# A hybrid decoder layer: TensorE's instructions in written order through the banded attention, with other banks for two of its tiles

## The chip, the core and the metric

The kernel runs on one core of one Trainium2 chip. The metric is the device time of one launch in microseconds. The core's engines work through queues of their own and wait for one another by semaphores: TensorE (PE in the profile) does matmuls and transposes into the accumulators (PSUM, eight banks of 128 x 512 float32), ScalarE (ACT) and VectorE (DVE) read these, GpSimd (POOL) does a little arithmetic and starts some DMAs, and SyncE (SP) starts the loads of the weights.

## What is computed

One layer of a decoder with 256 tokens of width 2048. The part that the change touches is the mixer:

```
c_q, c_kv, k_r, q_s, k_s, v_s, gates = split(h @ w_in)
q  = rms_norm(c_q) @ mla_w_q_up          # latent attention, dense and causal
kv = rms_norm(c_kv) @ mla_w_kv_up
o_a = mla_attention(q, kv, rope(k_r))
o_b = swa_attention(q_s, k_s, v_s, sinks, rel_table)
      # 32 query heads of 64 in 4 groups, one key and value head for each group,
      # window 128 in banded blocks, bias by distance, a learned sink in the softmax
y  = (sigmoid(gA) * (o_a @ w_o_mla) + sigmoid(gB) * (o_b @ w_o_swa)) @ w_out
```

Behind it come the residual sum, a norm and a feed-forward part with a short convolution; neither is touched. The results have to be those of float32, so each large product is made of three matmuls of operands that are split into a high and a low part (float32r): high x high, low x high, high x low.

## The kernel before

**Projections.** `gemm` computes 512 (or 320) columns of `h @ w_in` for both blocks of 128 tokens, over 16 slices of depth. Weights come in chunks of two slices (`wchunk`): a DMA into a tile raw, ScalarE's cast into whi (L129), VectorE's subtraction into wlo (L130), all from small rings of tiles; then 12 matmuls (`mm3`, L154 to L156) add into accg, two accumulator banks of the pool `pacc`, which has four. The other pools of banks are `pst` (tag "t", two) and `pss` (tag "s", two).

**Ticks.** After each chunk `gemm` calls `tick`, which runs the steps that `at(t, ...)` has put down for that tick. So the small work of the attention is written between the chunks of a projection that runs at the same time.

**The banded attention.** Sixteen units u of two heads each, four units to a group g. While the projection of the next group runs, the four units of a group come one by one, two ticks apart. Of a unit are written, in this order and at these ticks:

- `swa_qT` (L454 ff., tile xp): four transposes of the scaled queries, copied to x2 by ScalarE;
- `score` (tile s, L490 and L492): six matmuls; VectorE adds the bias and takes the maxima; then `stats`, `expo` (ScalarE's exponentials, L512) and `norm` (ScalarE L522, VectorE L524);
- `pt` (L471): twice three transposes of the probabilities, each group split by ScalarE (L233, tile pth) and VectorE (L234, tile ptl);
- `pv` (tile po, L538 to L541): four matmuls with the values, copied and added by ScalarE (L543) and VectorE (L546) to o.

**The latent part.** Behind the last group the same manner of work goes on beside the projections of c_q (cq), of c_kv with k_r (ck, kr), and of the gates B, columns 0 and 1 (`gate_b(0)`, `gate_b(1)`). `latent` copies the accumulator (L579), squares it in place for the norm (L580, with the accumulator as scratch), scales it (L587), and `tr` transposes it (L593): a tile cqT0, cqT1 or ckT in one bank takes two pairs of transposes, and behind each pair stands a split of what it wrote, ScalarE's high part (L236) and VectorE's low part (L237):

```
for j in range(2):
    for t in range(NT):
        pe.transpose(pt[:, j * 256 + t * P:j * 256 + (t + 1) * P], lat[t][...], ident)
    c = slice(j * 256, (j + 1) * 256)
    split_to(hi_t[p][:, c], lo_t[p][:, c], pt[:, c], gmat[...])
```

**What sets the order.** The program is written in the order of ticks, but a scheduler of the compiler places each engine's instructions; it lets work that it holds ready go ahead of work that waits. Only a `tc.manual_schedule(engines=...)` around a piece of the program makes it keep the written order for the engines named; before, that is used at the head alone, for VectorE, ScalarE and SyncE. An instruction that waits stops all that is behind it on its engine.

Of the kernel before, what the change touches and what calls it, by code (L numbers as in the profile page):

```python
# [11 lines left out]
F32 = mybir.dt.float32  # L12
F32R = mybir.dt.float32r
# [6 lines left out]
P = 128  # L20
# [21 lines left out]
def trunk_layer(ctx, tc, x, g_mix_post, g_ffn_post, w_in, w_q, w_kv, sinks, wo_a, wo_b, w_out, w_up, w_down,  # L42
# [9 lines left out]
    pacc = ctx.enter_context(tc.tile_pool(name="pacc", bufs=4, space=PS))  # L52
    pss = ctx.enter_context(tc.tile_pool(name="pss", bufs=2, space=PS))
    pst = ctx.enter_context(tc.tile_pool(name="pst", bufs=2, space=PS))
# [4 lines left out]
    def sb(pl, shape, name, dt=F32, tag=None, bufs=None):  # L59
        return pl.tile(shape, dt, name=name, tag=tag or name, **({"bufs": bufs} if bufs else {}))  # L60
# [73 lines left out]
    steps = defaultdict(list)  # L134
    now = [0]

    def at(t, *fs):
        steps[max(t, now[0])].extend(fs)

    def tick():  # L140
        for f in steps.pop(now[0], ()):
            f()
        now[0] += 1

    def drain():
        while steps:
            tick()
# [97 lines left out]
    def bias_load(u, q):  # L245
        b = bias_of[u] = sb(pb, [P, 2, 384], f"bias{u}", tag="bias", bufs=2)
        row = lambda n: bass.AP(strip.tensor, strip.offset + 2 * u * 384, [[1, P], [384, 2], [1, n]])
        q.dma_start(b[:, :, 0:256], row(256))
        q.dma_start(b[:, :, 256:384], row(128))
# [196 lines left out]
    def swa_q(g, acc):  # L446

        qx_of[g] = []
        for t in range(NT):
            q = sb(p1, [P, 8, 2, 64], f"qx{g}_{t}", F32R, tag="qx", bufs=2)  # L450
            a3 = acc[t].rearrange("p (a b) -> p a b", b=64)
            split_to(q[:, :, 0, :], q[:, :, 1, :], a3, r1s[:, t:t + 1])
            qx_of[g].append(q)

    def swa_qT(u):

        qx, i = qx_of[u // 4], u % 4
        pt = pst.tile([P, 512], F32R, name=f"xp{u}", tag="t")
        for j in range(2):
            for t in range(NT):  # L460
                pe.transpose(pt[:, (j * 2 + t) * P:(j * 2 + t + 1) * P],
                             qx[t][:, 2 * i + j, :, :].rearrange("p a b -> p (a b)"), ident_r)
        xt = sb(p1, [P, 512], f"x2{u}", F32R, tag="x2", bufs=3)
        act.copy(xt, pt.bitcast(F32))
        xs_of[u] = xt

    def p_transpose(p, dst, tag):

        pt = pst.tile([P, 512], F32, name=f"pt{tag}", tag="t")
        for j, c in enumerate((2, 0, 1)):  # L470
            pe.transpose(pt[:, j * P:(j + 1) * P], p[:, c * P:(c + 1) * P], ident)  # L471
        split_to(dst[0], dst[1], pt[:, 0:384])

    def swa_unit(u, t0):

        g = u // 4
        h0 = 2 * u
        st = {}

        def load():  # L480
            if u > 1:
                bias_load(u, pool)
            st["bias"] = bias_of[u]
            st["p"] = sb(p1, [P, 2, 384], f"p{u}", tag="p", bufs=3)
            st["mx"] = sb(p1, [P, 2, 2], f"mx{u}", tag="mx", bufs=3)

        def score(i):
            sp = pss.tile([P, 512], F32, name=f"s{u}_{i}", tag="s")
            q = xs_of[u][:, i * 256:(i + 1) * 256]
            pe.matmul(sp[:, 0:256].rearrange("p (a b) -> p a b", a=2), q[:, 0:P], kx[g][:, :, P:2 * P], start=True, stop=True)  # L490
            for w in (1, 0):
                pe.matmul(sp[:, 256:512], q[:, P:2 * P], kx[g][:, w, P:384], start=w == 1, stop=w == 0)  # L492
            p, bias, mx = st["p"][:, i, :], st["bias"][:, i, :], st["mx"]
            vec.tensor_tensor(p[:, 0:P], sp[:, P:256], bias[:, 0:P], op=ALU.add)
            vec.tensor_tensor_reduce(p[:, P:384], sp[:, 256:512], bias[:, P:384], op0=ALU.add, op1=ALU.min, scale=-1.0, scalar=-NEG, accum_out=mx[:, i, 1:2])
            vec.tensor_tensor_reduce(p[:, 0:P], p[:, 0:P], sp[:, 0:P], op0=ALU.add, op1=ALU.min, scale=-1.0, scalar=-NEG, accum_out=mx[:, i, 0:1])

        def stats():
            mx = st["mx"]
            sk = sink[:, h0:h0 + 2].unsqueeze(2).to_broadcast([P, 2, 2])  # L500
            vec.tensor_tensor(mx, mx, sk, op=ALU.min)
            if u == 0:
                sb(p1, [P, 24], "pad_d")
            st["e"] = sb(p1, [P, 2, 2], f"e{u}", tag="e", bufs=3)
            vec.tensor_tensor(st["e"], mx, sk, op=ALU.subtract)
            st["sm"] = sb(p1, [P, 2, 2], f"sm{u}", tag="sm", bufs=3)
            act.activation(st["e"], st["e"], AF.Exp)

        def expo(i):
            pb = st["p"]  # L510
            for t, (a, b) in enumerate(((0, 128), (128, 384))):
                act.activation(pb[:, i, a:b], pb[:, i, a:b], AF.Exp, bias=st["mx"][:, i, t:t + 1], scale=-1.0,  # L512
                               accum_out=st["sm"][:, i, t:t + 1])

        def norm():
            pb, sm = st["p"], st["sm"]
            vec.tensor_tensor(sm, sm, st["e"], op=ALU.add)
            vec.reciprocal(sm, sm)
            for i in range(2):
                for t, (a, b) in enumerate(((0, 128), (128, 384))):  # L520
                    if i:
                        act.activation(pb[:, i, a:b], pb[:, i, a:b], AF.Copy, scale=sm[:, i, t:t + 1])  # L522
                    else:
                        vec.tensor_scalar(pb[:, i, a:b], pb[:, i, a:b], sm[:, i, t:t + 1], None, op0=ALU.mult)  # L524

        def pt(i):
            if i == 0:
                st["pt"] = [sb(p1, [P, 2, 384], f"pt{part}{u}", F32R, tag="pt" + part, bufs=2) for part in "hl"]
            p_transpose(st["p"][:, i, :], [w_[:, i, :] for w_ in st["pt"]], f"{u}_{i}")

        def pv():

            st["po"] = pst.tile([P, 512], F32, name=f"po{u}", tag="t")
            st["o"] = sb(p1, [P, 256], f"o{u}", tag="o", bufs=2)
            v0, v1 = (vx[t][:, g, :, :].rearrange("p a b -> p (a b)") for t in range(NT))
            po = st["po"].rearrange("p (a b) -> p a b", a=2)
            ph, pl_ = st["pt"]
            pe.matmul(po, v0, ph[:, :, P:384], start=True, stop=False)  # L538
            pe.matmul(po[:, :, P:256], v1, ph[:, :, 0:P], start=False, stop=False)
            pe.matmul(po[:, :, P:256], v1, pl_[:, :, 0:P], start=False, stop=False)  # L540
            pe.matmul(po, v0, pl_[:, :, P:384], start=False, stop=True)  # L541
            cr = sb(p1, [64, 512], f"cr{u}", tag="cr", bufs=1)
            act.copy(cr, st["po"][64:128, :])  # L543
            for j in range(2):
                c = slice(j * 256, (j + 1) * 256)
                vec.tensor_tensor(st["o"][j * 64:(j + 1) * 64, :], st["po"][0:64, c], cr[:, c], op=ALU.add)  # L546
            act.copy(OH(u), st["o"])
            pool.tensor_tensor(OL(u), st["o"], OH(u).bitcast(F32), op=ALU.subtract)

        at(t0 - (3 if u > 1 else 1), load)  # L550
        at(t0, lambda: score(0), lambda: score(1))
        at(t0 + 1, stats, lambda: expo(0), lambda: expo(1), norm)
        at(t0 + 3, lambda: pt(0), lambda: pt(1))
        at(t0 + 4, pv)

    for g in range(4):
        if g:
            more_raw[:] = late
            accq, _ = gemm(XH, XL, w_in, 0, KT, C_QS + 512 * g, 512)
        else:  # L560
            kv_evac(acckv)
        swa_q(g, accq)
        b = now[0]
        for i in range(4):
            at(b + 1 + 2 * i, lambda u=4 * g + i: swa_qT(u))
            swa_unit(4 * g + i, b + 2 + 2 * i)


# [40 lines left out]
    acc, _ = gemm(XH, XL, w_in, 0, KT, 0, 512)  # L609
# [4 lines left out]
    acc, _ = gemm(XH, XL, w_in, 0, KT, C_KV, KVR + ROPE)  # L614
# [38 lines left out]

    tb = {0: gate_b(0), 1: gate_b(1)}
    drain()
    es1.close()
    esb.close()

# [143 lines left out]
    b = now[0] + 42  # L802
# [11 lines left out]
    for j in range(4):  # L814
        acc, _ = gemm(XH, XL, w_in, 0, KT, C_GA + 512 * j, 512)
        for t in range(NT):
            g = stg(f"ta{j}_{t}")
# [48 lines left out]
    for j in range(4):  # L866
        ld = merge_loads(j)
        acc, _ = gemm(AH, AL, wo_a, 0, KT, 512 * j, 512)
        for t in range(NT):
            a, b = ld[t]  # L870
# [63 lines left out]
    for b in range(4):  # L934
        c0, n = W_BLOCKS[b]
        last = b == 3
        acc, todo = gemm(MH_, ML_, w_out, 0, KT, c0, n, split=0 if last else None, extra={i: (px,) for i in range(EXTRA)} if last else None)
# [115 lines left out]
    for j in range(4):  # L1053
        acc, _ = down(0, 24, 512 * j, 512)
# [32 lines left out]
    for b in range(4):  # L1087
# [5 lines left out]
        acc, todo = down(24, 20, 512 * b, 512, split=5 if last else None)  # L1093
# [74 lines left out]
```

## Time and profile before

| | before |
|---|---|
| median of 3 runs | 1477.67 us (1477.65 to 1477.79) |
| the profiled execution's own time | 1478.18 us |
| its span, first to last instruction | 1476.4 us |
| TensorE busy | 1463.9 us, 99% of the span |
| VectorE, ScalarE, GpSimd busy | 66%, 54%, 4% |
| mean granted clock of TensorE | 0.998 |
| the banded attention, 50.89 to 195.56 us | 144.67 us, ScalarE busy 84% of it |

The profile is that of one execution. Busy time is the time in which an engine had an instruction in work; a matmul's record is longer than its share of the stream, since matmuls overlap, so a price per matmul is read from the distance of two starts. A wait has a length and a releaser, the instruction whose end let it go. Stretches are given in microseconds from the first instruction.

### The profile page before, as it was taken

What the parts mean: (1) busy time and instruction counts of PE and PEld (TensorE: products, weight loads), DVE (VectorE), ACT (ScalarE), POOL (GpSimd) and SP (SyncE); (2) the same over time, 40 slices, a digit from 0 to 9 for tenths busy, and PEclk for the clock granted to TensorE, in tenths of its full rate; (3) what the DMA queues carried; (4) which work ended last, traced back from release to release, by engine and by line L of the source; (5) the groups of instructions that cost most, each with busy time, mean ns of one, the idle gap of its engine ahead of it and who ended that gap; (6) DMA issues with size and microseconds to landing.
All of it is one profiled execution on the core that took longest, in us unless ns stands there. A gap on an engine that the chain in (4) does not pass through costs nothing.

```text
span 1476.4 us, 20927 instructions
## 1 busy us (share of the span) xinstructions
PE 1463.9 (99%) x7694; PEld 1255.4 (85%) x7694; DVE 973.5 (66%) x1730; ACT 804.1 (54%) x1328; POOL 54.3 (4%) x88
## 2 busy tenths in 40 slices
PE   9999999999999999999999999999999999999997
PEld 7888888888899988888888888888888888888886
DVE  7688784445667665655777687776444676688555
ACT  7588864434565554344665465554443555555443
POOL 0022200000000010000000000000000000000000
PEclk9999999999999999999999999999999999999999
DMA  9665566666655557776655655656555655655653
GB/s 350 191 174 137 134 196 197 203 211 200 186 160 155 176 168 244 260 238 225 200 172 171 210 181 186 191 181 207 197 189 190 191 178 182 214 186 184 201 195 119
DMA packets 160935, 285.41 MB, mean 193 GB/s; under 512 B 18560, under 2 KB 31488, under 8 KB 160704
## 3 DMA queue, kind: packets, MB, share of 16 engines
q1 hardware_dynamic: 155904, 268.45, 56.9%
q0 software_dynamic: 4496, 14.95, 4.1%
q8 instruction: 60, 0.98, 0.3%
q10 hardware_dynamic: 432, 0.68, 0.1%
q14 instruction: 43, 0.35, 0.1%
HBM read 277.74 MB, written 6.29 MB: 192 GB/s over the span
## 4 chain that ended last, share of the span: by engine, by line
PE 97%; ACT 1%; DMA 1%; DVE 1%; SPq 0%; issue 0%; DVEq 0%; ACTq 0%
PE accg L154 18%; PE accg L156 18%; PE accg L155 18%; PE accb L195 11%; PE acca L195 10%; PE accb L203 6%; PE acca L203 5%; PE acckv L339 1%; PE accq L339 1%; PE mpo L790 1%; PE ms L756 1%; PE pt L471 1%; PE qn L721 1%; PE qn L720 1%; PE qn L719 1%; PE s L492 0%
## 5 line engine op out<-in xcount | busy, mean ns | idle before, releaser
L130 DVE TENSOR_TENSOR wlo<-raw,whi 128x1024 fp32r<-128x1024 f32 (+1 forms) x484 | 587.4, 1217 | 426.6 <-ACT whi L129 400.1
L129 ACT CAST whi<-raw 128x1024 fp32r<-128x1024 f32 (+1 forms) x484 | 506.6, 1048 | 542.3 <-PE accg L156 318.7
L154 PE MATMUL accg<-whi,ah 128*128 128x512 f32 (+1 forms) x800 | 312.4, 391 | 0.0
L155 PE MATMUL accg<-wlo,ah 128*128 128x512 f32 (+1 forms) x800 | 310.4, 388 | 0.0
L156 PE MATMUL accg<-whi,al 128*128 128x512 f32 (+1 forms) x800 | 310.0, 387 | 0.0
L156 PEld LDWEIGHTS accg<-whi,al 128*128 128x128 f32 x800 | 150.2, 188 | 29.8
L155 PEld LDWEIGHTS accg<-wlo,ah 128*128 128x128 f32 x800 | 150.4, 188 | 27.7
L154 PEld LDWEIGHTS accg<-whi,ah 128*128 128x128 f32 x800 | 150.4, 188 | 27.4
L154 PE MATMUL accg<-whi,bh 128*128 128x512 f32 x272 | 106.6, 392 | 0.0
L156 PE MATMUL accg<-whi,bl 128*128 128x512 f32 x272 | 106.1, 390 | 0.0
L155 PE MATMUL accg<-wlo,bh 128*128 128x512 f32 x272 | 106.0, 390 | 0.0
L195 PE MATMUL accb<-bh,whi 128*128 128x512 f32 x352 | 84.2, 391 | 0.0
L195 PE MATMUL accb<-bl,whi 128*128 128x512 f32 x352 | 84.0, 390 | 0.0
L195 PEld LDWEIGHTS accb<-bh,whi 128*128 128x128 f32 x352 | 65.2, 188 | 13.3 <-ACT rfrow L931 0.3
L195 PEld LDWEIGHTS accb<-bl,whi 128*128 128x128 f32 x352 | 65.2, 188 | 13.0
L195 PE MATMUL acca<-bh,whi 128*128 128x512 f32 x320 | 76.2, 390 | 0.0
L195 PE MATMUL acca<-bl,whi 128*128 128x512 f32 x320 | 76.1, 390 | 0.0
L195 PEld LDWEIGHTS acca<-bh,whi 128*128 128x128 f32 x320 | 59.4, 188 | 12.2 <-DVE ds L1056 0.3
L195 PEld LDWEIGHTS acca<-bl,whi 128*128 128x128 f32 x320 | 59.4, 188 | 11.9
L156 PEld LDWEIGHTS accg<-whi,bl 128*128 128x128 f32 x272 | 51.1, 188 | 10.7
L154 PEld LDWEIGHTS accg<-whi,bh 128*128 128x128 f32 x272 | 51.1, 188 | 10.3
L155 PEld LDWEIGHTS accg<-wlo,bh 128*128 128x128 f32 x272 | 51.1, 188 | 10.2
(333 smaller groups left out, 1999.1 us busy)
## 6 DMA issues: line engine op xcount, KB each, us to landing
raw<-in_ffn_w_up_dram SPq DMA_DIRECT2D x176, 512.0 KB, 4.4
raw<-in_w_in_dram SPq DMA_DIRECT2D x96, 512.0 KB, 4.4
raw<-in_ffn_w_down_dram SPq DMA_DIRECT2D x88, 512.0 KB, 3.9
raw<-in_w_o_swa_dram SPq DMA_DIRECT2D x32, 512.0 KB, 4.3
raw<-in_w_o_mla_dram SPq DMA_DIRECT2D x32, 512.0 KB, 4.4
raw<-in_w_out_dram SPq DMA_DIRECT2D x32, 512.0 KB, 4.3
wxr<-in_w_in_dram SPq DMA_DIRECT2D x13, 512.0 KB, 7.8
raw<-in_mla_w_q_up_dram SPq DMA_DIRECT2D x48, 128.0 KB, 2.8
```

What stands on the lines that cost most here:

```text
L129: act.copy(hi[:, :n], raw[:, :n])
L130: vec.tensor_tensor(lo[:, :n], raw[:, :n], hi[:, :n].bitcast(F32), op=ALU.subtract)
L154: pe.matmul(o, ah, bh, start=start, stop=False)
L155: pe.matmul(o, ah, bl, start=False, stop=False)
L156: pe.matmul(o, al, bh, start=False, stop=stop)
L195: pe.matmul(acc[i], hi[:, c:c + P], xs(kt), start=kt == 0, stop=kt == nk - 1)
L203: pe.matmul(acc[i][:, 0:256], lo[:, c:c + P], xs(k + 2 * n + j)[:, 0:256], start=False, stop=False)
L339: pe.matmul(o(a)[t][:, c], xs[x_][t], w_[:, 512 * a + c.start:512 * a + c.stop], start=start, stop=stop)
L471: pe.transpose(pt[:, j * P:(j + 1) * P], p[:, c * P:(c + 1) * P], ident)
L719: pe.matmul(o, wh, ch(k), start=k == 0, stop=False)
L720: pe.matmul(o, wh, cl(k), start=False, stop=False)
L721: pe.matmul(o, wl, ch(k), start=False, stop=k == nk - 1)
```

## The change

`at` takes a turn, and a tick's steps run sorted by it. The query transposes of a unit (turn 1) move from one tick ahead of its scores to two ticks ahead (one for the first unit of a group), the value products get turn 2, and so an even tick writes the scores of one unit, the query transposes of the next and the value products of the unit two before, in this order. The tiles xp and po move from the pool `pst` to `pacc`, whose four banks also hold the running projection. And from the first group to behind `gate_b(1)` TensorE keeps the written order, in the latent part too; the other engines' order is still the scheduler's.

```diff
-    def at(t, *fs):
-        steps[max(t, now[0])].extend(fs)
+    def at(t, *fs, turn=0):
+        steps[max(t, now[0])].extend((turn, f) for f in fs)
...
-        for f in steps.pop(now[0], ()):
+        for _, f in sorted(steps.pop(now[0], ()), key=lambda e: e[0]):
             f()
...
-        pt = pst.tile([P, 512], F32R, name=f"xp{u}", tag="t")
+        pt = pacc.tile([P, 512], F32R, name=f"xp{u}", tag="acc")
...
-            st["po"] = pst.tile([P, 512], F32, name=f"po{u}", tag="t")
+            st["po"] = pacc.tile([P, 512], F32, name=f"po{u}", tag="acc")
...
-        at(t0 + 4, pv)
-
+        at(t0 + 4, pv, turn=2)
+
+    written = ExitStack()
+    written.enter_context(tc.manual_schedule(engines={mybir.EngineType.PE}))
     for g in range(4):
...
-            at(b + 1 + 2 * i, lambda u=4 * g + i: swa_qT(u))
+            at(b + (2 * i if i else 1), lambda u=4 * g + i: swa_qT(u), turn=1)
             swa_unit(4 * g + i, b + 2 + 2 * i)
...
     tb = {0: gate_b(0), 1: gate_b(1)}
     drain()
+    written.close()
```

First place, TensorE in a steady unit of the second group. Before, the two groups of probability transposes of unit 4 stand with a matmul of the projection between them, and behind ten more come the query transposes of unit 6, a matmul again and the value products (a name's number is its unit or chunk; the last number is the tile's own):

```order
L471 MATMUL pt4_0_1245<-ident_105,p4_1016 128x128 x3
L154 MATMUL accg_8_0_967<-whi14_1286,ah6_142 128x512
L471 MATMUL pt4_1_1251<-ident_105,p4_1016 128x128 x3
L155 MATMUL accg_8_0_967<-wlo14_1287,ah6_142 128x512
...
L461 MATMUL xp6_1272<-ident_r_110,qx1_0_961 128x128
L461 MATMUL xp6_1272<-ident_r_110,qx1_1_964 128x128
...
L156 MATMUL accg_8_1_968<-whi14_1286,al6_150 128x512
L538 MATMUL po4_1302<-pth4_1243,vx0_583 128x512
L539 MATMUL po4_1302<-pth4_1243,vx1_584 128x2x128
```

Now the even tick's bunch holds the scores of unit 6, the transposes of unit 7 (the two rows left out repeat the two shown) and the products of unit 4, and a whole chunk of 12 accg follows:

```order
L156 MATMUL accg_8_1_970<-whi14_1288,al6_150 128x512
L490 MATMUL s6_0_1304<-kx1_580,x26_1220 128x256
L492 MATMUL s6_0_1304<-kx1_580,x26_1220 128x256 x2
L490 MATMUL s6_1_1311<-kx1_580,x26_1220 128x256
L492 MATMUL s6_1_1311<-kx1_580,x26_1220 128x256 x2
L461 MATMUL xp7_1318<-ident_r_110,qx1_0_963 128x128
L461 MATMUL xp7_1318<-ident_r_110,qx1_1_966 128x128
...
L538 MATMUL po4_1325<-pth4_1252,vx0_583 128x512
L539 MATMUL po4_1325<-pth4_1252,vx1_584 128x2x128
L540 MATMUL po4_1325<-ptl4_1253,vx1_584 128x2x128
L541 MATMUL po4_1325<-ptl4_1253,vx0_583 128x512
```

The six pt of a unit stand together in the odd tick in the same way; small work that was spread over some five places of a unit is at two.

Second place, TensorE where the latent part's transposes stand. Before, the first pair of cqT0 and the second of cqT1 share a place, other matmuls stand between the pairs of one tile, and the second pair of cqT0 follows a chunk and a half later:

```order
L156 MATMUL accg_32_1_2250<-whi38_2472,al6_150 128x320
L540 MATMUL po15_2422<-ptl15_2391,vx1_584 128x2x128
L541 MATMUL po15_2422<-ptl15_2391,vx0_583 128x512
L593 MATMUL cqT0_2434<-ident_105,cq0_2227 128x128
L593 MATMUL cqT0_2434<-ident_105,cq1_2230 128x128
L593 MATMUL cqT1_2461<-ident_105,cq0_2227 128x128
L593 MATMUL cqT1_2461<-ident_105,cq1_2230 128x128
L154 MATMUL accg_32_0_2249<-whi38_2472,ah6_142 128x320
```

Now the four of cqT1 stand side by side behind the last matmul of chunk 37 (the two rows left out, the second pair, read as the first), with chunk 38 behind them:

```order
L156 MATMUL accg_32_1_2252<-whi37_2447,al5_149 128x320
L595 MATMUL cqT1_2463<-ident_105,cq0_2229 128x128
L595 MATMUL cqT1_2463<-ident_105,cq1_2232 128x128
...
L154 MATMUL accg_32_0_2251<-whi38_2474,ah6_142 128x320
L155 MATMUL accg_32_0_2251<-wlo38_2475,ah6_142 128x320
```

The same holds for cqT0, one chunk earlier, and for ckT, behind the last matmul of chunk 45.

Third place, ScalarE at the same transposes, whose high splits L236 are the first step to the second pair's release. Before, its queue there has the first split of cqT1 ahead of two casts, and the next two splits ahead of the cast of chunk 42:

```order
L236 ACTIVATE cqh_1808<-cqT1_2461,gx_123 128x256
L129 CAST whi40_2549<-raw40_2547 128x1024
L129 CAST whi41_2567<-raw41_2565 128x1024
L543 COPY cr15_2428<-po15_2422 64x512
L236 ACTIVATE cqh_1808<-cqT0_2434,gx_123 128x256
...
L129 CAST whi42_2585<-raw42_2583 128x1024
```

Now it reads:

```order
L236 ACTIVATE cqh_1810<-cqT0_2424,gx_123 128x256
L129 CAST whi40_2551<-raw40_2549 128x1024
...
L129 CAST whi41_2569<-raw41_2567 128x1024
L543 COPY cr15_2439<-po15_2433 64x512
L129 CAST whi42_2587<-raw42_2585 128x1024
L236 ACTIVATE cqh_1810<-cqT1_2463,gx_123 128x256
L547 CAST bh7_593<-o15_2434 128x256
```

The cast of chunk 42 has moved ahead of both splits of cqT1.

## Rows read from the trace of the kernel before

**Rows 1.** The page, engines: busy us, share of the span, instructions.

```profile
PE 1463.9 (99%) x7694; PEld 1255.4 (85%) x7694; DVE 973.5 (66%) x1730; ACT 804.1 (54%) x1328; POOL 54.3 (4%) x88
```

**Rows 2.** TensorE's waits: us in total, times, longest.

```profile
PE ckT L593 <- DVE ckx L237: 1.3, 1, 1.3
PE warm L69 <- DVE first L66: 1.1, 1, 1.1
```

**Rows 3.** Stretches: us, busy (x count) of five engines, clock, DMA share, GB/s.

```profile
50.89:195.56 144.67, 144.42 (x813) 122.84 (x812) 120.26 (x384) 121.92 (x316) 34.12 (x43) 1.00 0.59 158
215.00:222.00 7.00, 5.75 (x28) 4.42 (x27) 4.43 (x6) 3.89 (x5) 0.00 (x0) 1.00 0.76 232
222.00:361.00 139.00, 139.00 (x615) 115.09 (x614) 65.82 (x58) 58.80 (x59) 3.29 (x6) 1.00 0.65 204
...
1469.80:1476.40 6.60, 0.00 (x0) 0.00 (x0) 2.78 (x5) 0.00 (x0) 0.00 (x0) 0.50 0.43 160
```

**Rows 4.** TensorE's timeline of one unit: start, us, line, tiles, count.

```profile
100.35 0.46 PE L461 MATMUL xp<-ident_r,qx 128*128 128x128 f32 x4
100.65 0.47 PE L156 MATMUL accg<-whi,al 128*128 128x512 f32 x1
100.95 0.39 PE L538 MATMUL po<-pth,vx 128*128 128x512 f32 x1
...
101.64 0.40 PE L154 MATMUL accg<-whi,ah 128*128 128x512 f32 x1
...
103.26 0.28 PE L490 MATMUL s<-kx,x 128*128 128x256 f32 x1
...
103.98 0.40 PE L155 MATMUL accg<-wlo,ah 128*128 128x512 f32 x1
...
105.14 0.49 PE L471 MATMUL pt<-ident,p 128*128 128x128 f32 x3
105.39 0.48 PE L154 MATMUL accg<-whi,ah 128*128 128x512 f32 x1
105.71 0.49 PE L471 MATMUL pt<-ident,p 128*128 128x128 f32 x3
105.95 0.48 PE L155 MATMUL accg<-wlo,ah 128*128 128x512 f32 x1
106.27 0.39 PE L156 MATMUL accg<-whi,al 128*128 128x512 f32 x1
...
108.35 0.46 PE L461 MATMUL xp<-ident_r,qx 128*128 128x128 f32 x4
```

**Rows 5.** Timeline of all engines at ckT, accg left out; idle before, releaser.

```profile
215.55 0.38 PE L593 MATMUL ckT<-ident,ck 128*128 128x128 f32 x2
...
217.19 1.05 ACT L129 CAST whi<-raw 128x1024 fp32r<-128x1024 f32 x1 [0.84 <-DMA raw<-in_w_in_dram]
...
218.15 0.47 ACT L236 ACTIVATE ckx<-ckT,gx 128x256 fp32r<-128x256 f32 x1
218.27 1.23 DVE L130 TENSOR_TENSOR wlo<-raw,whi 128x1024 fp32r<-128x1024 f32 x1 [0.67 <-ACT whi L129]
219.42 0.48 DVE L237 SCALAR_TENSOR_TENSOR ckx<-ckT,gx,ckx 128x256 fp32r<-128x256 f32 x1
...
219.95 0.33 PE L593 MATMUL ckT<-ident,ck 128*128 128x128 f32 x1 [1.25 <-DVE ckx L237]
```

**Rows 6.** Timelines of ScalarE and VectorE in the latent part.

```profile
183.28 0.58 ACT L580 ACTIVATE accg<-cq 128x512 f32<-128x512 f32 x1
...
190.62 0.88 DVE L587 TENSOR_SCALAR cq<-cq,cq_y 128x512 f32<-128x512 f32 x2
```

**Rows 7.** The page, DMA issues: count, KB each, median us to landing.

```profile
raw<-in_w_in_dram SPq DMA_DIRECT2D x96, 512.0 KB, 4.4
```

**Rows 8.** TensorE's timeline at the head.

```profile
4.20 1.19 PE L339 MATMUL acckv<-whi,ah 128*128 128x256 f32 x4
...
5.81 0.63 PE L339 MATMUL acckv<-wlo,ah 128*128 128x512 f32 x2
6.28 0.64 PE L339 MATMUL accq<-whi,ah 128*128 128x256 f32 x4
```

## The prediction

> **What bounds the kernel now.** I read the page's busy list first: TensorE is busy in 99% of the span [rows 1]. The list of TensorE's waits says the same from the other side: over 1476 us its only wait of more than a microsecond, apart from that for the first operand at the start, is 1.3 us ahead of the second pair of ckT transposes, released by VectorE's low-part split [rows 2]. So time is added wherever TensorE is made to wait, and is won only where its own stream gets denser; there is no slack later that could swallow either. The table of stretches shows where the change acts: from 50.89 to 195.56 us, the banded attention beside the projections, TensorE is busy in 144.42 of 144.67 us, ScalarE in 121.92 (84%) and VectorE in 120.26; the plain gate projections behind it, 222 to 361 us, run 615 matmuls in 139.00 us, 0.226 us each, at granted clock 1.00 [rows 3].
>
> **What the bunches can win.** One steady unit of two heads is read from TensorE's timeline, from one query transpose xp to the next: 100.35 to 108.35, 8.00 us [rows 4]. In it stand 24 accg matmuls of 512 columns (24 x 0.226 = 5.42) and 20 small ones, which take the other 2.58. The group of four po goes by without loss (100.95 to 101.64, 0.69), and so do the six s (103.26 to 103.98, 0.72). A loss shows where accg follows transposes: the accg behind xp holds the engine for 0.30 us (100.65 to 100.95), and those behind pt for 0.32 (105.39 to 105.71, and 105.95 to 106.27), where 0.226 is usual [rows 4]. After the change a unit has two bunches, s-xp-po and pt-pt. The accg behind xp goes, but then po stands behind xp; one of two accg behind pt goes, but the first group of three pt takes only 0.25, so that some of the 0.09 is merely time of the transposes shown at the next instruction. I take 0.1 us a unit, 1.5 us for 16 units. The ends: nothing, and, if everything above the small groups' own pace went (xp 0.30, pt 2 x 0.25, s 0.72, po 0.69 and 5.42, together 7.63 of 8.00), 0.37 x 16 = 5.9. **Term: -1.5 (0 to -5.9).**
>
> **Does a fixed order make TensorE wait inside the units?** With the order written, everything queued behind a waiting instruction waits too, accg included. I followed each small group to what makes its operand. s needs ScalarE's copy of xp, which now has two chunks of accg instead of one (a chunk is 12 x 0.226 = 2.7 us). po stands one chunk and a bunch's start behind pt, about 3.9 us, and needs two splits on ScalarE and VectorE, some 1.4 us beyond pt. pt stands more than a chunk behind the normalisation. By the durations of one unit I get 2.5 us to spare ahead of po and 3.7 ahead of pt. The banks: xp and po now use the two accumulator banks that the running projection doesn't hold, and at each of three group ends the next projection takes both. It then waits for the xp copy and for po's two adds; there I count 0.3 to 0.9 us to spare. So zero for the units and group ends; if the cover is short, that is the third rival.
>
> **Where I expect waits: the latent part, with its pairs.** The four transposes of cqT0, cqT1 and ckT each stand in two pairs in one bank: the second pair is written only when ScalarE's high and VectorE's low split of the first have read it. Before, the scheduler put other matmuls between the pairs: in all three cases but ckT enough, at ckT one chunk, and 1.25 us were missing. There the whole chain can be read: pair one at 215.55; ScalarE's weight cast at 217.19, queued ahead, then the high split at 218.15; VectorE's weight split at 218.27, then the low split at 219.42; pair two at 219.95 [rows 5]. Now the four stand side by side, and TensorE pays the chain itself, three times.
>
> - **cqT0**: ScalarE's and VectorE's queues hold its splits right behind earlier work, with no weight chunk that waits for TensorE. The bare chain is 0.47 + 0.48 [rows 5] and about 0.25 of handing over and of the pair itself: **+1.2** (1.2 to 2.3, with another cast of 1.05 ahead).
> - **cqT1**: ahead of its high split ScalarE has the cast of chunk 42, which needs a ring slot that chunk 37 frees, and the last matmul of chunk 37 stands directly ahead of cqT1. So cast 1.05, weight split 1.23 and low split 0.48, about 2.7 [rows 5]. Chunk 42's data can be later still: a load takes 4.4 us to land [rows 7] and is issued when VectorE is done with chunk 39; by that I get 3.75. **+3.2** (1.2 to 4.5).
> - **ckT**: again the cast of a chunk (50) is queued ahead of the split, and needs the slot of chunk 45, whose last matmul is directly ahead of ckT. By the row above 2.7 if the data is there. In the trace the cast started only at 217.19, on data, and by the same chain the wait would be 4.2; but the two waits at cqT give the loads several us to catch up. 2.7 less the 1.25 of before: **+1.45** (-0.05 to +2.95).
>
> Two more that the fixed order uncovers. **po13** takes a bank that the projection cq held and that ScalarE still uses as scratch for the squares (0.58 us each, behind the two casts and in turn with exponentials [rows 6]); I get the first square 0.9 us after TensorE comes to po13: **+1.0** (0 to 1.5). **pt15** needs the normalisation of unit 15, which VectorE does behind the two scalings of cq (0.88) [rows 6]; before, the scheduler had let accg pass: **+0.3** (0 to 1.0).
>
> Outside this stretch TensorE's order is the same, and the moved steps (query transposes, value products) issue no DMA, so nothing is counted there or on SyncE's and GpSimd's queues. The bank moves alone cost nothing: the two banks that xp and po leave serve pt, kT and krT alone.
>
> **Sum**: -1.5 + 1.2 + 3.2 + 1.45 + 1.0 + 0.3 = +5.65 us on the profiled 1478.18 gives 1483.8; the median of the runs, 1477.67, stands 0.5 below the profiled one, so **1483.3 us**. The waits alone lie between +2.3 (three bare chains less 1.25) and +12.
>
> **Rivals.** (1) *The clock falls in the new waits.* It was 1.00 through ckT's 1.25 us, and 0.50 behind the last matmul, 1469.80 to 1476.40 [rows 3]. What a fall costs is bounded by the head: TensorE's first work follows a wait of 1.1 us [rows 2], four 256-column matmuls take 0.99 us from 4.20, and from 5.81 two of 512 take 0.47, the full rate [rows 8]. At most 4.7 us at half rate, 2.3 lost a fall; one or two make 1485.6 to 1487.9. A wait of 3 us is longer than any that I saw at full clock, but matmuls are dense on both sides of it. [...] Chance 0.10. (2) *The chains are short*: the other engines run ahead, po13 and pt15 are free, each pair waits the bare 1.2: 3 x 1.2 - 1.25 - 1.5 = +0.85, 1478.5, no change. For it speaks that ScalarE's queue order is the scheduler's, with idle time in the tail; against it, both casts named above need TensorE's last chunk. 0.17. (3) *ScalarE falls behind in the units*: it is used 84% on the mean, and if each unit is 0.3 us late for po or pt, 16 x 0.3 = 4.8 comes on top of the waits: 1488. It decides once the 2.5 us ahead of po is used up. 0.07. (4) *The dense stream wins*: 4.5 to 5.9 us from the bunches with bare chains gives 1477.67 + 2.35 - 5.2 = 1474.8, and lower only if a chain is hidden: the other side. It decides if a change between small and large matmuls costs 0.3 us a unit instead of 0.1. 0.06.
>
> **How the numbers follow.** Forecast 0.60, rivals 0.10, 0.17, 0.07, 0.06. What the measurement can tell from no change is about 0.2%, 3 us: faster means below 1474.7, slower above 1480.6. Rival 4 is half faster, half same; the forecast's lower tail (waits near 1.2 with po13 free) adds 0.03 to same. Faster 0.04, same 0.21, slower 0.75. The range leaves out rival 4, the lower half of rival 2, and the far ends of 3: 1478 to 1488.
>
> **What would show it.** In the profile after: TensorE's waits list cqT twice and ckT once, released by VectorE's low split, of 1 to 4 us each, and po13 released by ScalarE's square; a unit takes 7.9 instead of 8.00 us; no wait at s, xp, po, pt of units 1 to 12; PEclk 1.00 behind each wait. I am wrong if the waits sum to under 3 us, if the unit shrinks by over 0.25, or if waits show inside the units.

## The result and the profile after

The changed kernel takes **1488.95 us** (median of 6 runs, 1487.38 to 1490.29) where the kernel before takes 1477.73 (median of 6, beside them): ratio **1.0072**, 95% interval 1.0062 to 1.0082. It is slower, as forecast, but by 11.2 us where 5.65 was forecast, and 0.95 us beyond the upper end of the range.

The profiled execution took 1487.67 us. Its busy list, beside that of [rows 1], shows the same work and a longer span, 1485.9:

```profile
PE 1464.7 (99%) x7694; PEld 1259.1 (85%) x7694; DVE 979.3 (66%) x1730; ACT 803.4 (54%) x1328; POOL 56.9 (4%) x88
```

TensorE's list of waits, which had one row behind the head in [rows 2], has four behind it now (us in total, times, longest; the row of warm is the head's):

```profile
PE cqT L595 <- DVE cql L237: 5.0, 2, 3.9
PE ckT L595 <- DVE ckx L237: 2.6, 1, 2.6
PE po L538 <- ACT accg L582: 2.5, 1, 2.5
PE warm L69 <- DVE first L66: 1.1, 1, 1.1
PE pt L471 <- DVE p L524: 0.4, 1, 0.4
```

They are the five waits that were forecast, and no other: none stands at s, xp, po or pt of units 1 to 12. A steady unit takes 7.89 us from one xp to the next, where 7.9 was forecast and 8.00 stood in [rows 4]:

```profile
100.33 0.46 PE L461 MATMUL xp<-ident_r,qx 128*128 128x128 f32 x4
108.22 0.46 PE L461 MATMUL xp<-ident_r,qx 128*128 128x128 f32 x4
```

The stretches say what the waits' list can't. The columns are those of [rows 3]; the last but two is the granted clock. The stretch 181.30 to 185.40 lies behind the wait of po13, 201.80 to 205.20 behind the one at cqT1, and 226.70 to 230.00 behind the one at ckT:

```profile
50.89:195.56 144.67, 140.70 (x793) 122.19 (x792) 125.38 (x385) 120.28 (x314) 36.41 (x43) 0.99 0.61 156
181.30:185.40 4.10, 4.10 (x17) 3.90 (x18) 3.36 (x16) 3.21 (x10) 0.00 (x0) 0.59 0.23 65
201.80:205.20 3.40, 3.40 (x14) 3.40 (x15) 0.48 (x1) 0.47 (x1) 0.01 (x1) 0.50 0.55 167
226.70:230.00 3.30, 3.30 (x16) 2.75 (x17) 0.48 (x1) 0.60 (x2) 0.00 (x0) 1.00 0.54 164
```

Behind two of the three long waits TensorE's granted clock is 0.59 over 4.1 us and 0.50 over 3.4; behind the third it is 1.00. The price can be read from single matmuls. Behind cqT1 an accg of 320 columns takes 0.267 us from start to start (202.39, 202.65, 202.92) where 0.147 is usual in the same projection (six take 0.88 from 196.33 to 197.21). In the wait ahead of it, from 198.00 to 201.70, TensorE is busy for 0.02 of 3.70 us, though the accg of chunk 38 stand next in its written order. Summed over the instructions of each stretch, I estimate a fall at about 1.65 us, 3.3 for the two.

```profile
201.68 0.65 PE L595 MATMUL cqT<-ident,cq 128*128 128x128 f32 x2 [3.94 <-DVE cql L237]
201.97 0.61 PE L154 MATMUL accg<-whi,ah 128*128 128x320 f32 x1
202.39 0.47 PE L155 MATMUL accg<-wlo,ah 128*128 128x320 f32 x1
202.65 0.47 PE L156 MATMUL accg<-whi,al 128*128 128x320 f32 x1
202.92 0.47 PE L154 MATMUL accg<-whi,ah 128*128 128x320 f32 x1
```

Where the time went is best seen from the first matmuls of the projections, which stand in the same order in every kernel. The table gives when each starts, counted from the first accg of the first projection (50.90 us before, 49.95 after: the head of this execution happened to be 0.95 shorter), and how often the clock fell between the head and the end. The waits are counted below it as gaps, what two starts lie apart beyond the usual distance. All kernels of the experiments below are in it; it is worked out from TensorE's timeline of each profiled execution.

| kernel | ck and kr | gates 0 | gates 1 | last matmul | falls of the clock |
|---|---|---|---|---|---|
| before | 127.28 | 147.75 | 172.09 | 1415.94 | 0 |
| after | 125.98 | 157.06 | 182.40 | 1426.29 | 2 |
| e1, written order only through group 3 | 125.97 | 148.07 | 174.73 | 1418.61 | 1 |
| e2, four transposes, then splits | 125.96 | 150.68 | 173.21 | 1417.11 | 1 |
| e3, waits filled | 125.98 | 157.03 | 183.96 | 1427.82 | 2 |
| e4, old banks | 134.99 | 160.12 | 185.43 | 1429.29 | 1 |
| e5, e2 and po13 later | 125.97 | 148.70 | 171.23 | 1415.07 | 0 |
| e6, before with four transposes, then splits | 127.27 | 148.02 | 170.56 | 1414.42 | 0 |
| e7, before with moved banks | 128.10 | 149.81 | 174.13 | 1417.99 | 0 |
| e8, e5 with old ticks | 131.76 | 156.73 | 179.26 | 1423.12 | 1 |
| e9, e1 and e2 | 125.98 | 147.90 | 170.43 | 1414.30 | 0 |
| e10, e9 with late po in old banks | 126.00 | 148.66 | 171.21 | 1415.07 | 0 |
| e11, po13 later only | 125.99 | 150.99 | 177.92 | 1422.08 | 1 |

After against before: -1.30 up to the projection of ck and kr (won beside the units up to 12), then +10.61 up to gates 0 (po13, pt15, the two cqT, two falls), +1.00 up to gates 1 (ckT), and +0.04 in the remaining 1244 us. Together +10.35; the spans differ by 9.5, since the head was 0.95 shorter. The waits make 8.56 of it up to gates 0 (gaps of 2.69, 0.52, 1.25 and 4.10) and 1.32 behind (2.73 less the 1.41 of before), the falls 3.3; what is left, 10.35 - 13.18 = -2.8, I put down to the denser stream. It is a remainder, and no run measures it by itself.

### The profile page after: what moved, and what is told of

It reads as the page before. It is cut to its first block, busy times and chain, and to the rows that moved or that the text cites. A ratio compares the mean times of both kernels' runs of the same rounds, so it can differ in the third digit from the quotient of the medians.

```text
span 1485.9 us, 20958 instructions
## 1 busy us (share of the span) xinstructions
PE 1464.7 (99%) x7694; PEld 1259.1 (85%) x7694; DVE 979.3 (66%) x1730; ACT 803.4 (54%) x1328; POOL 56.9 (4%) x88
## 4 chain that ended last, share of the span: by engine, by line
PE 95%; DVE 2%; ACT 1%; DMA 1%; issue 0%; SPq 0%; DVEq 0%; ACTq 0%
PE accg L154 17%; PE accg L155 17%; PE accg L156 17%; PE accb L195 11%; PE acca L195 10%; PE accb L203 6%; PE acca L203 5%; PE accq L339 1%; PE acckv L339 1%; PE mpo L793 1%; PE ms L759 1%; DMA raw<-in_w_in_dram 1%; DVE wlo L130 1%; PE qn L724 1%; PE qn L723 1%; PE qn L722 1%
## 5 line engine op out<-in xcount | busy, mean ns | idle before, releaser
L156 PEld LDWEIGHTS accg<-whi,bl 128*128 128x128 f32 x272 | 51.1, 188 | 10.7
```

The costliest lines, as they stand in the source:

```text
L156: pe.matmul(o, al, bh, start=False, stop=stop)
```

## The experiments

Times are medians; ratios are against runs of the kernel before on the same chip, whose medians were 1478.0 (e1 to e4), 1477.98 (e5 to e8) and 1477.84 us (e9 to e11). Theory A is that of the prediction with the clock's falls: the tail of the attention and the latent part lose the time. The rivals say that the units lose it, or the banks, or that the clock is no part of it.

### e1: the written order ends behind the third group

```diff
             swa_unit(4 * g + i, b + 2 + 2 * i)
+    written.close()
...
     drain()
-    written.close()
```

> The changed kernel, but the written order of TensorE ends behind the third group's loop: the last group's units that run beside the projection cq, and the latent part, are the scheduler's again; banks, turns and ticks stay. Theory A (the time is lost in the tail: pair waits 5.0 + 2.6 less the 1.25 of before, 2.9 at po13 and pt15, and two falls of the clock, 3.3; the bunches win about 2): these waits and falls go, units 1 to 11 keep their bunches, so 1475.5 to 1477.0 us, TensorE's waits at cqT under 0.3 us. Rival B (the fixed order or the moved banks cost inside the units): 1481 or more, with waits in the units.

Measured: **1478.25 us**, ratio 0.9999 (0.9989 to 1.0008). That is 1.25 us above the range of theory A. Still, 10.7 of the 11.2 us lie behind the third group's loop, and rival B falls: up to the projection of ck the kernel is as fast as the changed one (125.97). But the 1.3 us that it has won there don't come out at the end. Left with the scheduler's order it still has, in its profiled execution:

```profile
PE ckT L596 <- DVE ckx L237: 2.3, 1, 2.3
PE po L538 <- ACT accg L583: 1.3, 1, 1.3
```

The pair of ckT again, with a chunk between the two pairs as before, and po13 at the bank of cq. The profiled execution was the slowest of ten (1480.08), with a fall behind ckT (granted clock 0.94 over 200 to 230 us); the table's row is to be read with that. Beside cq, where TensorE has the scheduler's order again, e1 takes the same 31.58 us as the changed kernel (32.23 before): what is won there doesn't need the written order.

### e2: all four transposes, then the splits

```diff
             for j in range(2):
                 for t in range(NT):
                     pe.transpose(pt[:, j * 256 + t * P:...], ...)
+            for j in range(2):
                 c = slice(j * 256, (j + 1) * 256)
                 split_to(hi_t[p][:, c], lo_t[p][:, c], pt[:, c], ...)
```

> The changed kernel, but in the latent part all four transposes of a tile are written ahead of its two splits, so that the second pair need not wait for the split of the first in the same bank. Theory A: the waits at cqT0, cqT1 and ckT go (5.0 + 2.6) and with them the fall of the clock behind cqT1 (1.65); po13 stays with its 2.5 and its fall: 1488.95 - 9.2 = 1479.7 us (1478.5 to 1481). Rival C (the chain behind these transposes is itself late, and the waits come back at the next matmuls that need a cast or a bank): at most half is won, 1484 or more, with new waits at accg.

Measured: **1477.86 us**, ratio 0.9996 (0.9987 to 1.0006), 11.1 us under the changed kernel, more than expected. TensorE waits no more at cqT or ckT, and nothing came back at accg, so rival C falls:

```profile
PE po L538 <- ACT accg L582: 2.8, 1, 2.8
PE warm L69 <- DVE first L66: 1.1, 1, 1.1
PE pt L471 <- DVE p L524: 0.4, 1, 0.4
```

The pairs that share a bank are therefore the cause of the three waits and, with the clock, of most of the loss. po13's wait and a fall behind it (granted clock 0.93 over 175 to 200 us) are still there; e2 is level with the kernel before only because ckT's gap of 1.41 and what the stream wins pay for them. On the profiled executions the step is 9.2 us (1426.29 to 1417.11 in the table), as expected; the 1.9 more between the medians may come from other numbers of falls in the runs without a trace (the changed kernel's mean clock is 0.995 in two of six, 0.996 in the profiled one; e2's is 0.997 or 0.998 in nine, 0.996 in the profiled one). No trace shows it.

### e3: the two longest waits filled with matmuls

```diff
+    def fill(n):
+        fl = pst.tile([P, 512], F32, name="fl", tag="t")
+        for _ in range(n):
+            pe.matmul(fl[:, 0:256], XH(0)[:, 0:P], XH(0), start=True, stop=True)
...
         def pv():
+            if u == 13:
+                fill(18)
...
             for j in range(2):
+                if j and name == "cq" and p == 1:
+                    fill(28)
```

> The changed kernel with matmuls of 256 columns into an unused bank, which nothing reads, at the two longest waits: 18 ahead of po13 (18 x 0.119 = 2.1 us) and 28 between the two pairs of cqT1 (3.3 us). They are shorter than the waits of 2.53 and 3.94, so the waits' ends stay where they are. Theory A (the fall of the clock behind these waits costs 1.65 us each, and comes from TensorE standing idle): the clock stays at 1.00, 1488.95 - 3.3 = 1485.6 us (1484.5 to 1486.5). Rival D (the clock's fall is no consequence of the idle time, or costs nothing): 1488 to 1490 as before.

Measured: **1489.26 us**, ratio 1.0071 (1.0056 to 1.0086): as slow as the changed kernel. Half of the expectation held. The first two stretches are those of the filled waits, and the clock stays at 1.00 through them and over the 4 us behind them (182 to 186, 203 to 207); but the other two lie behind waits of 1.27 us at po14 and 2.6 at ckT, and there it is at 0.52 and 0.50:

```profile
179.00:182.00 3.00, 2.83 (x20) 2.59 (x21) 2.69 (x15) 3.00 (x11) 0.00 (x0) 1.00 0.00 0
200.00:203.00 3.00, 3.00 (x28) 3.00 (x27) 1.62 (x2) 1.63 (x3) 0.74 (x1) 1.00 0.49 169
189.60:192.10 2.50, 2.50 (x12) 2.50 (x11) 2.46 (x8) 1.28 (x3) 0.00 (x0) 0.52 0.50 144
227.40:230.10 2.70, 2.70 (x8) 2.08 (x7) 0.48 (x1) 0.17 (x1) 0.00 (x0) 0.50 0.59 190
```

TensorE, at a granted clock of 1.00 behind po13, came to po14 before VectorE had the low split ready:

```profile
188.91 0.39 PE L547 MATMUL po<-ptl,vx 128*128 128x256 f32 x1 [1.27 <-DVE ptl L234]
```

So the four falls of the changed kernel's execution and of this one all stand behind a wait, and at the two waits filled with matmuls that nobody reads the clock stayed at 1.00, where it had been 0.59 and 0.50 behind them; one execution of each doesn't show that idle time alone brings the fall. That a fall costs 1.65 us net this run doesn't show either: what TensorE won it lost again up to gates 0 (157.03 against 157.06 in the table), to the wait at po14 and the fall behind it, and at ckT the clock fell this time.

### e4: xp and po in their old banks

```diff
-        pt = pacc.tile([P, 512], F32R, name=f"xp{u}", tag="acc")
+        pt = pst.tile([P, 512], F32R, name=f"xp{u}", tag="t")
...
-            st["po"] = pacc.tile([P, 512], F32, name=f"po{u}", tag="acc")
+            st["po"] = pst.tile([P, 512], F32, name=f"po{u}", tag="t")
```

> The changed kernel with xp and po back in the two banks that pt uses; order and turns stay. Theory A (the moved banks are what lets a written order run without waits in the units): the second pt of a unit takes po's bank, whose two adds end about 3.5 us behind po, and waits 0.5 to 1.0 us in each of 16 units; po13's wait for the cq bank goes, with its fall of the clock (2.5 + 1.65): 1493 to 1501 us. Rival B (the banks don't matter in the units): no waits at pt, and 1485 us by the loss of po13's wait.

Measured: **1492.05 us**, ratio 1.0092 (1.0077 to 1.0107), 1 us short of the range expected. po13's wait goes as expected, but the units wait at another place than I named: not in each unit at pt, but at the three group ends, where xp follows pt in a bunch and takes the bank that pt has just filled.

```profile
PE xp L461 <- DVE ptl L234: 6.6, 3, 2.2
PE pt L471 <- ACT p L512: 0.8, 1, 0.8
PE pt L471 <- DVE p L524: 0.8, 1, 0.8
```

With the bunches of the change, where xp stands right behind pt at a group's end, the written order needs the moved banks; with them the units up to 12 run without a wait. The three waits at xp, of 2.16, 2.25 and 2.25 us, are alike, and the clock fell behind the first alone (the stretches behind the first two; behind the third it is 1.00, over 150 to 175 us):

```profile
91.90:95.20 3.30, 3.30 (x9) 2.52 (x9) 1.54 (x3) 1.19 (x3) 0.00 (x0) 0.50 0.91 308
126.90:130.30 3.40, 3.40 (x19) 2.90 (x20) 2.27 (x6) 1.79 (x5) 0.00 (x0) 1.00 0.47 164
```

### e5: e2, and unit 13's value products one tick later

```diff
-        at(t0 + 4, pv, turn=2)
+        at(t0 + (5 if u == 13 else 4), pv, turn=2)
```

> As e2 (all four transposes ahead of the two splits), and the value products of unit 13 one tick later, behind the transposes of unit 14, so that the projection's chunk and pt14 run while ScalarE squares cq in the bank that po13 takes. Theory A (po13's wait of 2.8 with the clock's fall behind it, 1.9, is all that e2 loses yet): the wait shrinks to 0.5 or less and the clock stays at 1.00: 1477.9 - 2.5 - 1.9 = 1473.5 us (1473 to 1475), faster than both kernels by what the bunches win. Rival E (ScalarE is late in any case in this stretch, and the wait moves to pt14, po14 or pt15): 1476.5 to 1478.

Measured: **1476.51 us**, ratio 0.9989 (0.9980 to 0.9998). po13's wait is gone and the clock does not fall (1.00 over 176 to 192 us, mean 0.999 in the profiled execution), but only 1.35 us are won on e2 where 4.4 were expected. Rival E has it right, in place and in size: the wait has moved on to the next small work that needs the other engines.

```profile
PE po L540 <- DVE ptl L234: 1.2, 2, 1.0
PE warm L69 <- DVE first L66: 1.1, 1, 1.1
PE pt L471 <- DVE p L524: 0.8, 2, 0.5
```

### e6: the kernel before with e2's edit alone

The edit is that of e2, made to the kernel before.

> The kernel before with one edit only: all four transposes of a tile ahead of its two splits. If the pairs in one bank are the cause of the wait at ckT, its 1.25 us go: 1478.0 - 1.25 = 1476.7 us, and TensorE has no wait over 0.3 us behind the head. If the wait is that of a late chunk in whatever order, it stays: 1478.0.

Measured: **1476.0 us**, ratio **0.9985** (0.9976 to 0.9994). TensorE has no wait over 0.3 us behind the head; the scheduler now puts the four transposes side by side, where no split stands between them:

```profile
215.43 0.60 PE L593 MATMUL ckT<-ident,ck 128*128 128x128 f32 x4
```

2.0 us are won where 1.25 stood in the list of waits and was expected. On the profiled executions it is 1.5 (1415.94 to 1414.42), the gap of 1.41 and little else.

### e7: the kernel before with the moved banks alone

The two lines of the diff on xp and po, with the scheduler's order and the old ticks.

> The kernel before with xp and po in the accumulator banks, and nothing else: the scheduler's order, the old ticks. Theory A (the banks alone win nothing, the bunches do): 1477 to 1479 us, the time from the first accg to the first of the projection behind cq within 0.5 us of before. Rival F (more banks let the scheduler place the small work better, and that is the gain): 1475 to 1476.5.

Measured: **1479.29 us**, ratio 1.0007 (0.9998 to 1.0016), 0.3 above the expected range and not to be told from no change. The banks alone win nothing: the projection of ck starts 0.82 us later than before (table; within 0.5 was expected), and po has a new wait of 1.3 us, `PE po L538 <- ACT pth L233`. Rival F falls.

### e8: e5 with the query transposes at their old ticks

```diff
-            at(b + (2 * i if i else 1), lambda u=4 * g + i: swa_qT(u), turn=1)
+            at(b + 1 + 2 * i, lambda u=4 * g + i: swa_qT(u))
```

> As e5, but the query transposes at their old ticks, behind the probability transposes and one tick ahead of their scores. Bunches are two a unit again (s and po, pt and xp), so if the written order is what wins: within 0.7 us of e5. Rival G (the query transposes need the two chunks of lead): the scores wait for the copy of xp, which ScalarE does behind the exponentials, 0.2 to 0.5 us in each of 16 units: e5 + 3 to 8 us.

Measured: **1482.78 us**, ratio 1.0033 (1.0021 to 1.0046), e5 + 6.3. Rival G has the size right and the place half: the copy of xp is what comes late, but mostly at the ends of groups, where the next projection needs xp's bank, four times, and at s only twice.

```profile
PE accg L154 <- ACT x L464: 4.7, 4, 1.6
PE cqT L595 <- DVE ptl L234: 2.2, 1, 2.2
PE s L490 <- ACT x L464: 1.3, 2, 0.9
```

The two ticks of lead that the change gives to the query transposes are part of what keeps the written order free of waits.

### e9 and e10: e1 and e2 together, and with the last value products in their old banks

e9 has the edits of e1 and of e2. e10 adds:

```diff
-            st["po"] = pacc.tile([P, 512], F32, name=f"po{u}", tag="acc")
+            st["po"] = (pst if u > 12 else pacc).tile([P, 512], F32, name=f"po{u}", tag="t" if u > 12 else "acc")
```

> e1 and e2 together: written order through the third group only, and all four transposes ahead of the two splits; the banks as in the changed kernel. ckT's wait of 2.3 and the fall of the clock behind it go from e1; po13's 1.3 and pt15's 0.3 stay: 1478.25 - 2.3 - 0.5 = 1475.5 us (1475 to 1476.2), about 0.5 below e6, by what the bunches of units 1 to 11 win (0.65 up to the third group's end) less po13. If the bunches win nothing, 1477, e6 plus po13's wait.

> e9 with the value products of units 13 to 15 in their old banks, so that po13 does not wait for the squares of cq. If po13's bank is the cause of its wait, it goes: 1475.5 - 1.3 = 1474.2 us (1474 to 1475.3), and TensorE has no wait over 0.5 us behind the head; if ScalarE is late in any case there, the wait stands at pt or po under another name, 1475.5.

Measured: e9 **1476.33 us**, ratio 0.9990 (0.9981 to 0.9999); e10 **1476.75 us**, ratio 0.9993 (0.9984 to 1.0001). Both miss their ranges, e9 by 0.1 us and e10 by 1.45. e9 gives what e6 gives, so the bunches of units 1 to 11 win nothing at the end, though they stand 1.3 us ahead at the projection of ck (table). In e10 the cause of po13's wait is gone and the wait is not: 1.3 us stand at pt, released by ScalarE's exponentials.

```profile
PE pt L471 <- ACT p L512: 1.3, 1, 1.3
```

What they seem to run into shows in one stretch, 176 to 184 us, of before, of after and of e9 in this order (columns as above; the fourth busy time is ScalarE's):

```profile
176.00:184.00 8.00, 8.00 (x58) 7.43 (x56) 5.96 (x25) 7.91 (x24) 0.73 (x1) 1.00 0.32 94
```

```profile
176.00:184.00 8.00, 5.47 (x30) 5.08 (x29) 5.62 (x26) 7.95 (x26) 0.74 (x1) 0.83 0.16 43
```

```profile
176.00:184.00 8.00, 6.71 (x48) 6.34 (x47) 5.57 (x25) 7.89 (x23) 0.74 (x1) 1.00 0.15 43
```

In these three executions ScalarE has work for 7.9 of 8.0 us (7.34 in e2's, 7.51 in e5's, 6.36 in e10's). It has the exponentials, copies and splits of the last units and both the copies and the squares of cq there. The kernel before is as full on ScalarE and yet doesn't wait: TensorE has 58 matmul records in the stretch, against 30 and 48, so its scheduler had other matmuls to put in. That ScalarE is what takes the lead away is argued from these rows; no run has less work on ScalarE there. Nor has any run the new ticks with the scheduler's order from the start, so what the written order alone wins in the units stays open.

### e11: the changed kernel with po13 later, and nothing else

The edit of e5, made to the changed kernel.

> The changed kernel with unit 13's value products one tick later and nothing else: the pairs as they are. po13's 2.5 and the fall of the clock behind it (1.65) go; by e5 about 1.5 comes back at pt14, pt15 and po14; the pairs' waits (5.0 + 2.6) stay: 1488.95 - 4.15 + 1.5 = 1486.3 us (1485 to 1488). If e5's small step from e2 (1.4) holds here too, 1487.5.

Measured: **1483.42 us**, ratio 1.0038 (1.0024 to 1.0052), 5.5 under the changed kernel where 2.65 was expected. The pairs' waits are there, but shorter at cqT: 3.6 for the two instead of 5.0, and only one fall is left in the profiled execution, behind ckT, with the same wait as in the changed kernel's, behind which the clock there stayed at 1.00 (a row of the timeline, and one of the stretches):

```profile
220.89 0.44 PE L595 MATMUL ckT<-ident,ck 128*128 128x128 f32 x2 [2.57 <-DVE ckx L237]
```

```profile
221.00:225.00 4.00, 4.00 (x12) 3.18 (x13) 0.48 (x1) 0.47 (x1) 0.00 (x0) 0.58 0.44 138
```

Its four runs on one chip fit a price of the clock: 1481.73 us at a mean granted clock of 0.999, 1483.01 and 1483.84 at 0.997, 1485.63 at 0.996. A thousandth of mean clock is by estimate 1.5 us of this span; from the first of these runs to the last it is 3.9 us for three thousandths, though two runs at 0.997 differ by 0.8 too.

## Why the prediction was wrong in size

- **Where and by what: right.** The five places, the releasers, the steady unit's 7.9 us and the absence of waits in units 1 to 12 came as forecast. e2 shows that the pairs in one bank are the cause of the three waits in the latent part; e1, that the written order beside the first three projections is not.
- **The bunches, -1.5**: the remainder above gives -2.8 of TensorE's time, of which 1.30 stand at the start of the projection of ck: 0.1 a unit, as forecast. The first three projections take 31.06, 31.58 and 31.77 us where 30.74, 31.74 and 32.58 stood before, together 0.66 less; 0.65 more is won beside cq. The other 1.5 lie behind, where the forecast counted the share of the last units alone. The size was right within the ends. That it would be a gain at all is another matter: e9 and e6 end alike.
- **cqT0 +1.2**: 1.08 in the trace. **ckT** 2.7 less 1.25: 2.57. **pt15** +0.3: 0.36.
- **cqT1 +3.2**: 3.94. The chain is the one named, with the late data that I had put at 3.75: the cast of chunk 42 waited 1.24 us for its load, and then all stood in the queue as said.

```profile
197.35 0.38 PE L595 MATMUL cqT<-ident,cq 128*128 128x128 f32 x2
...
198.92 1.04 ACT L129 CAST whi<-raw 128x1024 fp32r<-128x1024 f32 x1 [1.24 <-DMA raw<-in_w_in_dram]
199.99 0.47 ACT L236 ACTIVATE cqh<-cqT,gx 128x256 fp32r<-128x256 f32 x1
200.00 1.23 DVE L130 TENSOR_TENSOR wlo<-raw,whi 128x1024 fp32r<-128x1024 f32 x1 [0.91 <-ACT whi L129]
...
201.14 0.48 DVE L237 SCALAR_TENSOR_TENSOR cql<-cqT,gx,cqh 128x256 fp32r<-128x256 f32 x1
```

- **po13 +1.0 (0 to 1.5): the first term that failed, with 2.53.** The bank and the releaser were right. I had let ScalarE's queue run without a stop. In it the cast of unit 12's output stands ahead of the exponentials of unit 14 and of the copy of cq, and it waited 1.74 us for VectorE's adds, which stood behind the passes of unit 14's scores and a weight split. I had counted what is queued ahead on ScalarE, but not what the instructions ahead wait for on the other engine; 2.53 less 1.74 is 0.79, near the 0.9 of the forecast. This is read from the trace; no run removed that stop alone.

```profile
175.98 0.41 ACT L547 CAST bh<-o 128x256 fp32r<-128x256 f32 x1 [1.74 <-DVE o L546]
...
179.11 0.68 ACT L581 ACTIVATE cq<-accg,r 128x512 f32<-128x512 f32 x1
...
180.43 0.58 ACT L582 ACTIVATE accg<-cq 128x512 f32<-128x512 f32 x1
```

- **The clock: the second step that failed, and the larger.** The forecast's likeliest case left it at 1.00 and gave the falls a rival's 0.10; two came in the profiled execution, 3.3 us by the estimate above. The row on which I leaned, a wait of 1.25 us at full clock [rows 3, 5], spoke for waits of that length alone, and I had myself forecast one of 3.2. The fall came behind 3.94 us at cqT1 and behind 2.53 us at po13, and 2.57 us at ckT did not bring it here and did in e11. The price of 2.3 us at most was an estimate from the head, where four matmuls of 256 columns take 0.99 us [rows 8] at a granted clock that the profile gives as 1.00 (4.00 to 6.00 us); no run shows that this pace comes from a fall of the clock. The 1.65 that the matmuls show lies below it. Rival 1's upper end, 1487.9, came nearest to 1488.95, in part by luck: it took 2.3 us a fall, and it had po13's wait at 1.0.

Terms as they came: -2.8 + 1.1 + 3.9 + 1.3 + 2.5 + 0.4 + 3.3 = 9.7, against +10.35 in the profiled execution; the remaining 0.6 is that each gap is some 0.15 longer than the wait listed. The medians differ by 0.9 more than that; which of the unprofiled runs had further falls no trace shows. The chances also don't add as they were written: by the terms given, same is 0.23, faster 0.03 and slower 0.74, and nothing hangs on it.

## What to carry to other kernels

Before an engine gets a fixed order, look for places where it writes a bank, another engine reads it, and it writes the same bank again: here the scheduler hid most of the cost with what it put between (1.25 us were left), and in written order it was the whole chain of the other engines' queues. Moving the reads behind the last write (e6, one line, 1476.0 us) was worth as much by itself as together with the change of order at its best (e9, 1476.33). And a wait on TensorE can be dearer than its length: 4.1 us at a granted clock of 0.59 and 3.4 at 0.50 followed two of them here, about 1.65 us lost each by my estimate; give the case its full chance as soon as a forecast has waits longer than any that the trace shows at full clock.

## What the runs showed of the hardware that I had not expected

In these executions the clock's fall does not follow from the wait's length alone: behind the same wait of 2.57 us at ckT the granted clock was 1.00 in the changed kernel's execution and 0.58 over the next 4 us in e11's, in e4 it was 0.50 behind a wait of 2.16 us and 1.00 behind two of 2.25, and in e3 it was 0.52 behind a wait of 1.27 us, which followed one of 0.34 by less than 2 us. The change's runs spread over 2.9 us and e11's over 3.9 us, where ten runs of e6, without such waits, spread over 1.0.
